# Log gates of a hybrid GLA/SSD layer: one fp32 array and fp32 masked sums in place of a high and a low part

## The chip, the core and the metric

The kernel runs on one core of a Trainium2 chip. The metric is the device time of one execution in microseconds; lower is better. Three timed runs of the kernel before gave 1431.48, 1432.50 and 1433.24 us, median 1432.5 us.

## What is computed

One layer of a diffusion backbone over 512 latent tokens and 256 context tokens, width 1024. A modulated RMS norm gives `h`; one input projection feeds a gated linear attention branch (GLA, 4 heads, two directions) and a state-space branch (SSD, 4 groups, two directions); both are projected back, gated, merged and added, and a SwiGLU FFN follows. The change concerns the log gates of GLA:

```
def log_gate(lr, up, bias):
    pre = (lr @ up + bias).astype(jnp.float32)
    return heads(jax.nn.log_sigmoid(pre) / GLA_TAU, GLA_DK)
# in the scan of a chunk:
b = jnp.cumsum(gi, axis=1)                  # running sum of the log gates
diff = b[:, :, None] - b[:, None, :]
decay = jnp.exp(jnp.where(mask, diff, -jnp.inf))
# the context's state, per head:
jnp.einsum('blhk,blhv->bhkv', k * jnp.exp(b[:, -1:] - b), v)
```

The sums over tokens (running sums within blocks of 128 tokens, and sums over what lies after or before a token) are matrix products with masks of zeros and ones.

## The kernel before

All matrices are cut into blocks of 512 KB that stream from DRAM on the queue of SyncE (`load_raw`, L173, three buffers `raw`). ScalarE rounds each to fp32r (`whi`, L188) and VectorE, or GpSimd in the SSD part, subtracts to get the rest (`wlo`, L189); there are two buffers of each. A projection is then three fp32r passes per product: high by high, high by low, low by high. The same three buffers `raw` also take blocks of the modulation weights (`raw_ada`), which GpSimd multiplies and adds up (L341 to L345).

The order of the instructions on each engine is made when the program is built: a list scheduler with a model of times places them, with priorities from the program order and from `tc.high_priority()`; each engine then executes its list in order and waits at semaphores. A tile of a pool with n buffers waits until the tile n before it of the same tag has been read.

The stretch in question follows the first projections. `MS` and `U` hold the low-rank gate input and its weights. For two directions `d` and six token tiles `i` (L466 to L480), TensorE makes `pre` (L469, PSUM bank of the kind `sm`, of which there are four), ScalarE takes Abs, Exp and Ln (L471 to L473), VectorE makes the log gate `ge` (`e` in the code, L474), rounds it to fp32r as `gh` (L477) and subtracts to get `gl` (L478). SyncE's queue writes both to a DRAM array `gdr` (L479, L480).

Then come the step sizes of SSD, "the dt stage" below: transposes `dtT` (L488) into two `sm` banks, `dt_v` (L489), a chain between VectorE and ScalarE through `dt_e`, `dt_u`, `dt_lu`, `dt_cr`, `dt` and `dt_ln` (L497 to L519), `nA` (L521), a load of ScalarE's tables for Tanh (L455), `dt_aH` and `dt_aL` (L527, L529), masked products `cum` and `suf` (L533), a copy `cum` (L541), `ebias` (L558), transposes and copies `cumT` (L562, L564). Beside it TensorE works on the projections: r of head 0 (`r_r`), then q and k of head 1 (`l_q`, and `l_k` with `c_k` for the context tokens).

`gla_chain(h)` (L582) handles one head. For each direction it loads the head's part of `gdr` on GpSimd's queue (L592, tiles `g` of the tags `cva` and `cvt`, two buffers each), makes running sums `gc` (four blocks), `kx` (384 columns) and `ky` (256 and 128 columns), each as one fp32r pass over the high part and one over the low part; all products with `early` have the line number L577. `gcum` and `kd` come from them. Level products `lv`, diagonal products `dg` and state products `S` are fp32 products already. In the program's text the projections of head h+1 stand behind the chain of head h; the scheduler interleaves them.

`ssd_chain(g)` (L784) follows the same pattern for four groups: `E` tiles are broadcast from DRAM on SyncE's queue (L829, tag `E4`, four buffers), added and merged on VectorE (L830, L832), and TensorE makes `st`, `y`, `yi` and the transposes `yT`, while the projections of the next group (`xs`, `z`) and the projection back (`pa`, `pb`) fill in.

Of the kernel before, what the change touches and what calls it, by code (L numbers as in the profile page):

```python
# [7 lines left out]
F32 = mybir.dt.float32  # L8
F32R = mybir.dt.float32r
I32 = mybir.dt.int32  # L10
U8 = mybir.dt.uint8
AF = mybir.ActivationFunctionType
ALU = mybir.AluOpType

P = 128
# [9 lines left out]
DK = 128  # L25
# [18 lines left out]
M_ID, M_LE, M_GE, M_GT, M_LT, M_ONE = range(6)  # L44
# [85 lines left out]
def hybrid_layer_kernel(ctx: ExitStack, tc: tile.TileContext, x, xc, wts, vec, rows, up, msk, lvl, out):  # L130
    nc = tc.nc
# [10 lines left out]
    dr = ctx.enter_context(tc.tile_pool(name="dr", bufs=1, space=DRAM))  # L142
# [4 lines left out]
    def sm_bank(name):  # L147
        return ps.tile([P, 512], F32, tag="sm", name=name)
# [4 lines left out]
    mkr = cst.tile([P, 5, P], F32R, name="mkr")  # L153
# [71 lines left out]
    with tc.tile_pool(name="st", bufs=1) as st:  # L225
# [77 lines left out]
        for i in range(6):  # L303
# [5 lines left out]
            for half in range(2):  # L309
                pt = sm_bank(f"xT_{i}_{half}")  # L310
# [9 lines left out]
    pj = mix.enter_context(tc.tile_pool(name="pj", bufs=2))  # L320
    ch = mix.enter_context(tc.tile_pool(name="ch", bufs=1))
# [27 lines left out]
    def proj_cols(key, with_ctx):  # L349
        if key[0] in ("q", "k") and key[1:2] != (0,):  # L350
            for _ in range(2):
                some_ada()
        if key[0] in ("ga", "gb"):
            some_ada()
        hi, lo = load_w(key)
        nm = "_".join(map(str, key))
        lat = mm_bank("l_" + nm)
        cx = mm_bank("c_" + nm) if with_ctx else None
        for k in range(KD):
            st, sp = k == 0, k == KD - 1  # L360
            nc.tensor.matmul(lat, hi[:, k, :], hH[:, k, 0:SEQ], start=st, stop=False)
            nc.tensor.matmul(lat, hi[:, k, :], hL[:, k, 0:SEQ], start=False, stop=False)
            if with_ctx:
                nc.tensor.matmul(cx[:, 0:CTX], hi[:, k, :], hH[:, k, SEQ:NT], start=st, stop=False)
                nc.tensor.matmul(cx[:, 0:CTX], hi[:, k, :], hL[:, k, SEQ:NT], start=False, stop=False)
            nc.tensor.matmul(lat, lo[:, k, :], hH[:, k, 0:SEQ], start=False, stop=sp)
            if with_ctx:
                nc.tensor.matmul(cx[:, 0:CTX], lo[:, k, :], hH[:, k, SEQ:NT], start=False, stop=sp)
        return lat, cx
# [91 lines left out]
        return gla_proj_vr(h, *gla_proj_qk(h))  # L461


    gdr = dr.tile([P, 2, 2, 6, 512], F32, name="gdr")

    for d in range(2):  # L466
        for i in range(6):
            pt = sm_bank(f"pre_{d}_{i}")
            nc.tensor.matmul(pt, MS[d][:, i * P:(i + 1) * P], U[:, d, :], start=True, stop=True)  # L469
            e = ch.tile([P, 512], F32, tag="s2", name=f"ge_{d}_{i}", bufs=7)  # L470
            nc.scalar.activation(e, pt, AF.Abs)  # L471
            nc.scalar.activation(e, e, AF.Exp, scale=-1.0)
            nc.scalar.activation(e, e, AF.Ln, bias=1.0)  # L473
            nc.vector.scalar_tensor_tensor(e, pt, 0.0, e, ALU.min, ALU.subtract)  # L474
            gh = ch.tile([P, 512], F32R, tag="z", name=f"gh_{d}_{i}", bufs=4)
            gl = ch.tile([P, 512], F32R, tag="E4", name=f"gl_{d}_{i}", bufs=4)
            nc.vector.tensor_copy(gh, e)  # L477
            nc.vector.tensor_tensor(gl, e, gh.bitcast(F32), ALU.subtract)  # L478
            nc.sync.dma_start(gdr[:, d, 0, i, :], gh.bitcast(F32))  # L479
            nc.sync.dma_start(gdr[:, d, 1, i, :], gl.bitcast(F32))  # L480


    dsh = [P, 6, 64]
# [1 line left out]
    for b, i0, n in ((0, 0, 4), (1, 4, 2)):  # L485
        pt = sm_bank(f"dtT_{b}")
# [6 lines left out]
    def dt_tile(name):  # L493
        return ch.tile(dsh, F32, tag="s2", name=name, bufs=7)

    e = dt_tile("dt_e")
# [63 lines left out]
    for d in range(2):  # L560
        pt = sm_bank(f"cumT_{d}")
# [6 lines left out]
    pr = gla_proj(0)  # L568


    class Early:


# [6 lines left out]
    early = Early()  # L580

    def gla_chain(h, qT, vt, kt, kT, rw, oH, oL):  # L582
        def s2(name, shape=(P, SEQ)):
            return ch.tile(list(shape), F32, tag="s2", name=f"{name}_{h}", bufs=7)

        cm, kd = [], []
        for d, mc, ms, n0, far, near in ((0, M_LE, M_GT, 0, 4, 5), (1, M_GE, M_LT, 1, 5, 4)):
            tag = ("cva", "cvt")[d]
            gp = []
            for p_ in range(2):  # L590
                gd = pj.tile([P, 6, DK], F32R, tag=tag, name=f"g_{h}_{d}_{p_}")
                nc.gpsimd.dma_start(gd, gdr[:, d, p_, :, h * DK:(h + 1) * DK])  # L592
                gp.append(gd)

            pt = sm_bank(f"gc_{h}_{d}")
            for n in range(NCH):
                for p_ in range(2):
                    early.matmul(pt[:, n * P:(n + 1) * P], gp[p_][:, n, :], mkr[:, mc - 1, :], start=(p_ == 0), stop=(p_ == 1))
            c_ = s2(f"gcum{d}")
            nc.scalar.activation(c_, pt, AF.Copy, scale=1.0 / TAU)  # L600
            cm.append(c_)

            px = sm_bank(f"kx_{h}_{d}")
            for p_ in range(2):
                early.matmul(px[:, 0:384], mkr[:, ms - 1, :], gp[p_][:, n0:n0 + 3, :], start=(p_ == 0), stop=(p_ == 1))
            py = sm_bank(f"ky_{h}_{d}")
            o0 = (far - 4) * P
            for p_ in range(2):
                early.matmul(py[:, 0:256], mkr[:, ms - 1, :], gp[p_][:, 4:6, :], start=(p_ == 0), stop=False)
            for p_ in range(2):  # L610
                early.matmul(py[:, o0:o0 + P], mkr[:, M_ONE - 1, :], gp[p_][:, near, :], start=False, stop=(p_ == 1))
            kk = pj.tile([P, 5, DK], F32, tag=tag, name=f"kd_{h}_{d}")
            nc.scalar.activation(kk[:, 0:3, :], px[:, 0:384].rearrange("p (i c) -> p i c", c=DK), AF.Exp, scale=1.0 / TAU)
            nc.scalar.activation(kk[:, 3:5, :], py[:, 0:256].rearrange("p (i c) -> p i c", c=DK), AF.Exp, scale=1.0 / TAU)
            nc.vector.tensor_tensor(kk[:, 0:3, :], kk[:, 0:3, :], kt[:, n0:n0 + 3, :], ALU.mult)
            nc.vector.tensor_tensor(kk[:, 3:5, :], kk[:, 3:5, :], kt[:, 4:6, :], ALU.mult)
            kd.append(kk)
# [12 lines left out]
        for d, order in ((0, (0, 1, 2, 3)), (1, (3, 2, 1, 0))):  # L630
            n0 = 0 if d == 0 else 1
            pt = sm_bank(f"S0_{h}_{d}")
# [3 lines left out]
            for a_, b_ in zip(order[:-1], order[1:]):  # L636
                pt = sm_bank(f"S_{h}_{d}_{b_}")
# [5 lines left out]
        pt = sm_bank(f"dg_{h}")  # L643
# [6 lines left out]
        for li, c in enumerate(LEVELS):  # L650
# [19 lines left out]
            pt = sm_bank(f"lv_{h}_{c}")  # L670
# [22 lines left out]
        for n in range(NCH):  # L693
# [4 lines left out]
            pt = pt2[:, (n % 2) * DV:(n % 2 + 1) * DV]  # L698
# [193 lines left out]

    oH0, oL0 = back_pair("oT_0")
    gla_chain(0, *pr, oH0, oL0)
    pr = gla_proj(1)
    gla_chain(1, *pr, oH0, oL0)
    pr = gla_proj(2)
    early_gate()
    proj_back(lambda c: ("pa", 0, c), oH0, oL0, acc_a, True)
    oH1, oL1 = back_pair("oT_1")  # L900
    gla_chain(2, *pr, oH1, oL1)
    pr = gla_proj(3)
    early_gate()
# [23 lines left out]
    for j in range(n_early[0], 8):  # L927
        ya = pj.tile([P, SEQ], F32, tag="cva", name=f"ya_{j}")
        nc.sync.dma_start(ya, ydr[:, j, :])
        lat, _ = proj_cols(("ga", j), False)  # L930
# [3 lines left out]
        lat, _ = proj_cols(("gb", j), False)  # L934
# [6 lines left out]
    pt = sm_bank("adaT")  # L941
# [72 lines left out]
    for i in range(4):  # L1014
# [14 lines left out]
        for half in range(2):  # L1029
# [3 lines left out]
            pt = sm_bank(f"hT_{i}_{half}")  # L1033
# [23 lines left out]
    for j0, nj in [(0, 2)] + [(j, 1) for j in range(2, NFF)]:  # L1057
# [12 lines left out]
        for j in js:  # L1070
            if nj == 2:
                f = sml.tile([P, SEQ], F32, tag="snw", name=f"f_{j}", bufs=1)
            else:
                f = fp.tile([P, SEQ], F32, tag="f32", name=f"f_{j}", bufs=2)
# [9 lines left out]
    pt = sm_bank("adaT2")  # L1084
# [130 lines left out]
```

## Time and profile before

| | value |
|---|---|
| median of three runs | 1432.5 us (1431.48 to 1433.24) |
| the profiled execution: its own time | 1428.55 us |
| its span, first to last instruction | 1426.7 us |
| TensorE busy | 1349.4 us (95%), 7462 products |
| VectorE busy | 881.1 us (62%) |
| ScalarE busy | 496.7 us (35%) |
| GpSimd busy | 476.1 us (33%) |
| mean granted TensorE clock | 0.986 of full speed |

The busy shares are means over stages that have different limits, so the rows are read by stretch: which engine is full there, and which wait of TensorE ends last. In a timeline row the numbers are start (us), length (us), engine, line, operation, and in brackets the idle time just before it on its engine with the instruction that ended it. Products are pipelined: the length of one holds its way through the array, so what a product costs TensorE is read from one start to the next, or from the length of a merged row (x8) against its count. An fp32 product appears as two records, an fp32r pass as one.

### The profile page before, as it was taken

How to read it: one execution, taken by the hardware profiler on the slowest of the kernel's cores; microseconds unless marked ns; L12 is line 12 of the kernel's file. 1: busy time of each engine (PE TensorE's matmuls, PEld its weight loads, DVE VectorE, ACT ScalarE, POOL GpSimd, SP SyncE). 2: the span in 40 equal slices, each digit the busy share in tenths (PEclk: the TensorE clock that was granted, in tenths of full speed). 3: DMA queues.
4: the chain of work that ended last, by engine and by line, in shares of the span. 5: the costliest groups of instructions: out<-in, count | busy, mean ns of one | idle time of the engine just before them, and what ended most of it. 6: DMA issues, size and time to landing. Idle time of an engine off the chain costs nothing.

```text
span 1426.7 us, 19130 instructions
## 1 busy us (share of the span) xinstructions
PE 1349.4 (95%) x7462; PEld 1146.0 (80%) x7462; DVE 881.1 (62%) x1317; ACT 496.7 (35%) x825; POOL 476.1 (33%) x341
## 2 busy tenths in 40 slices
PE   5888999999998999998999989999889999999997
PEld 3687999889888778876887787778678888888886
DVE  4599757583595588558857975767683343433235
ACT  6464343433434132532332342332333323232222
POOL 1346555245423533343353324114641122100001
PEclk9998999999999999999999999999999999999999
DMA  9375433423422423323322333457423343333331
GB/s 370 123 259 151 128 102 111 126 93 126 122 75 67 141 98 101 97 73 90 104 82 89 96 97 101 158 184 267 135 87 109 113 122 115 120 116 93 100 106 72
DMA packets 71386, 175.49 MB, mean 123 GB/s; under 512 B 6384, under 2 KB 22912, under 8 KB 71168
## 3 DMA queue, kind: packets, MB, share of 16 engines
q1 hardware_dynamic: 57056, 161.11, 34.6%
q0 software_dynamic: 13952, 12.79, 3.8%
q8 instruction: 59, 0.97, 0.3%
q10 hardware_dynamic: 288, 0.36, 0.1%
q14 instruction: 31, 0.25, 0.1%
HBM read 159.37 MB, written 14.87 MB: 122 GB/s over the span
## 4 chain that ended last, share of the span: by engine, by line
PE 66%; DVE 16%; DMA 9%; issue 5%; ACT 2%; POOL 1%; SPq 0%; POOLq 0%; DVEq 0%; ACTq 0%
DMA E<-cdr 6%; PE up L1069 3%; PE gate L1068 3%; PE gate L1069 3%; PE up L1068 3%; PE gate L1067 3%; PE up L1067 3%; DVE E L830 3%; PE db L204 3%; PE db L206 3%; PE db L205 3%; PE lv L577 2%; PE pb_pb L716 2%; PE pb_pb L715 2%; PE pb_pb L717 2%
## 5 line engine op out<-in xcount | busy, mean ns | idle before, releaser
L341 POOL TENSOR_TENSOR raw_ada<-raw_ada,cs 128x1024 f32<-128x1024 f32 x32 | 69.7, 2180 | 265.3 <-DMA raw_ada<-in_wts_dram 230.4
L830 DVE TENSOR_TENSOR E<-E,ebias 128x512 f32<-128x512 f32 x64 | 68.8, 1077 | 51.0 <-DMA E<-cdr 50.8
L343 POOL TENSOR_TENSOR raw_ada<-raw_ada 128x512 f32<-128x512 f32 x64 | 80.0, 1250 | 3.7
L386 PE MATMUL r_z<-whi_z,hH 128*128 128x256 f32 x256 | 74.6, 291 | 5.8 <-DVE z L781 3.0
L388 PE MATMUL r_z<-whi_z,hL 128*128 128x256 f32 x256 | 73.4, 287 | 0.0
L387 PE MATMUL r_z<-wlo_z,hH 128*128 128x256 f32 x256 | 73.0, 285 | 0.0
L1067 PE MATMUL gate<-h2H,whi_gate 128*128 128x512 f32 (+1 forms) x192 | 72.2, 376 | 0.0
L1068 PE MATMUL gate<-h2L,whi_gate 128*128 128x512 f32 (+1 forms) x192 | 72.1, 376 | 0.0
L1069 PE MATMUL gate<-h2H,wlo_gate 128*128 128x512 f32 (+1 forms) x192 | 71.9, 374 | 0.0
L189 POOL TENSOR_TENSOR wlo_xs<-raw_xs,whi_xs 128x1024 fp32r<-128x1024 f32 x16 | 40.6, 2536 | 75.3 <-ACT whi_xs L188 75.3
L1069 PE MATMUL up<-h2H,wlo_up 128*128 128x512 f32 x160 | 63.0, 394 | 0.0
L1068 PE MATMUL up<-h2L,whi_up 128*128 128x512 f32 x160 | 62.4, 390 | 0.0
L1067 PE MATMUL up<-h2H,whi_up 128*128 128x512 f32 x160 | 62.3, 389 | 0.0
L189 DVE TENSOR_TENSOR wlo_down<-raw_down,whi_down 128x1024 fp32r<-128x1024 f32 x18 | 22.1, 1225 | 62.4 <-ACT whi_down L188 62.3
L189 DVE TENSOR_TENSOR wlo_gate<-raw_gate,whi_gate 128x1024 fp32r<-128x1024 f32 x20 | 31.7, 1584 | 45.6 <-ACT whi_gate L188 45.6
L170 POOL TENSOR_TENSOR rr_f<-rv_f,negh 128x1 f32<-128x1 f32 x4 | 2.6, 662 | 168.5 <-DVE rv_f L168 168.5
L386 PE MATMUL r_v<-whi_v,hH 128*128 128x256 f32 x192 | 56.4, 294 | 0.0
L189 POOL TENSOR_TENSOR wlo_z<-raw_z,whi_z 128x1024 fp32r<-128x1024 f32 x16 | 39.6, 2475 | 49.2 <-ACT whi_z L188 36.6
L387 PE MATMUL r_v<-wlo_v,hH 128*128 128x256 f32 x192 | 55.5, 289 | 0.0
L715 PE MATMUL pb_pb<-yT,whi_pb 128*128 128x512 f32 x128 | 55.3, 434 | 0.0
L388 PE MATMUL r_v<-whi_v,hL 128*128 128x256 f32 x192 | 55.3, 288 | 0.0
L205 PE MATMUL db<-wlo_down,fH 128*128 128x512 f32 x142 | 55.3, 389 | 0.0
(479 smaller groups left out, 4446.7 us busy)
## 6 DMA issues: line engine op xcount, KB each, us to landing
raw_ada<-in_wts_dram SPq DMA_DIRECT2D x32, 512.0 KB, 4.0
E<-cdr SPq DMA_DIRECT2D x64, 256.0 KB, 3.5
raw_gate<-in_wts_dram SPq DMA_DIRECT2D x22, 512.0 KB, 3.7
raw_up<-in_wts_dram SPq DMA_DIRECT2D x22, 512.0 KB, 3.5
raw_down<-in_wts_dram SPq DMA_DIRECT2D x22, 512.0 KB, 3.5
aw<-in_wts_dram SPq DMA_DIRECT2D x8, 1024.0 KB, 15.5
raw_xs<-in_wts_dram SPq DMA_DIRECT2D x16, 512.0 KB, 3.5
raw_z<-in_wts_dram SPq DMA_DIRECT2D x16, 512.0 KB, 3.6
```

Source lines behind the costliest of these rows:

```text
L189: (nc.gpsimd if split_pool[0] else nc.vector).tensor_tensor(lo, raw, hi.bitcast(F32), ALU.subtract)
L205: nc.tensor.matmul(out_, aH, bL, start=False, stop=False)
L341: nc.gpsimd.tensor_tensor(raw, raw, cs[:, :, 0:1].to_broadcast([P, KD, P]), ALU.mult)
L343: nc.gpsimd.tensor_tensor(raw[:, 0:n, :], raw[:, 0:n, :], raw[:, n:2 * n, :], ALU.add)
L386: nc.tensor.matmul(o, hH[:, kk, tk], hi[:, k, :], start=st, stop=False, skip_group_check=True)
L387: nc.tensor.matmul(o, hH[:, kk, tk], lo[:, k, :], start=False, stop=False, skip_group_check=True)
L388: nc.tensor.matmul(o, hL[:, kk, tk], hi[:, k, :], start=False, stop=sp, skip_group_check=True)
L715: nc.tensor.matmul(pt, hi[:, k, cl], aH[:, k, :], start=(k == 0), stop=False)
L830: nc.vector.tensor_tensor(ed, ed, ebias[:, d, n, hh].unsqueeze(2).to_broadcast([P, EH, P]), ALU.add)
L1067: nc.tensor.matmul(pts[kj][:, tk], hi[:, k, :], h2H[:, k, tk], start=(k == 0), stop=False)
L1068: nc.tensor.matmul(pts[kj][:, tk], hi[:, k, :], h2L[:, k, tk], start=False, stop=False)
L1069: nc.tensor.matmul(pts[kj][:, tk], lo[:, k, :], h2H[:, k, tk], start=False, stop=(k == KD - 1))
```

## The change

The log gate is written once, as fp32, and read once. `gh`, `gl` and their tiles are gone; `gdr` has half the size; each masked sum is one fp32 product whose mask is the same array read as fp32. Nothing else is edited (`gates_end` is set and not used).

```
-    gdr = dr.tile([P, 2, 2, 6, 512], F32, name="gdr")
+    gdr = dr.tile([P, 2, 6, 512], F32, name="gdr")
...
-            nc.scalar.activation(e, e, AF.Ln, bias=1.0)
+            gates_end = nc.scalar.activation(e, e, AF.Ln, bias=1.0)
             nc.vector.scalar_tensor_tensor(e, pt, 0.0, e, ALU.min, ALU.subtract)
-            gh = ch.tile([P, 512], F32R, tag="z", name=f"gh_{d}_{i}", bufs=4)
-            gl = ch.tile([P, 512], F32R, tag="E4", name=f"gl_{d}_{i}", bufs=4)
-            nc.vector.tensor_copy(gh, e)
-            nc.vector.tensor_tensor(gl, e, gh.bitcast(F32), ALU.subtract)
-            nc.sync.dma_start(gdr[:, d, 0, i, :], gh.bitcast(F32))
-            nc.sync.dma_start(gdr[:, d, 1, i, :], gl.bitcast(F32))
+            nc.sync.dma_start(gdr[:, d, i, :], e)
...
+    def mkf(m):
+        return mkr[:, m - 1, :].bitcast(F32)
...
-            gp = []
-            for p_ in range(2):
-                gd = pj.tile([P, 6, DK], F32R, tag=tag, name=f"g_{h}_{d}_{p_}")
-                nc.gpsimd.dma_start(gd, gdr[:, d, p_, :, h * DK:(h + 1) * DK])
-                gp.append(gd)
+            gd = pj.tile([P, 6, DK], F32, tag=tag, name=f"g_{h}_{d}")
+            nc.gpsimd.dma_start(gd, gdr[:, d, :, h * DK:(h + 1) * DK])
...
-                for p_ in range(2):
-                    early.matmul(pt[:, n * P:(n + 1) * P], gp[p_][:, n, :], mkr[:, mc - 1, :], start=(p_ == 0), stop=(p_ == 1))
+                early.matmul(pt[:, n * P:(n + 1) * P], gd[:, n, :], mkf(mc), start=True, stop=True)
...
-            for p_ in range(2):
-                early.matmul(px[:, 0:384], mkr[:, ms - 1, :], gp[p_][:, n0:n0 + 3, :], start=(p_ == 0), stop=(p_ == 1))
+            early.matmul(px[:, 0:384], mkf(ms), gd[:, n0:n0 + 3, :], start=True, stop=True)
...
-            for p_ in range(2):
-                early.matmul(py[:, 0:256], mkr[:, ms - 1, :], gp[p_][:, 4:6, :], start=(p_ == 0), stop=False)
-            for p_ in range(2):
-                early.matmul(py[:, o0:o0 + P], mkr[:, M_ONE - 1, :], gp[p_][:, near, :], start=False, stop=(p_ == 1))
+            early.matmul(py[:, 0:256], mkf(ms), gd[:, 4:6, :], start=True, stop=False)
+            early.matmul(py[:, o0:o0 + P], mkf(M_ONE), gd[:, near, :], start=False, stop=True)
```

The scheduler makes a new order from it. Three places of it matter below. The first is the end of the gates and the start of the dt stage. On VectorE there stand before (the number behind a name is a serial number; line numbers behind L480 are lower in the changed kernel):

```order
L474 SCALAR_TENSOR_TENSOR ge_4_608<-pre_4_606,ge_4_608 128x512
L474 SCALAR_TENSOR_TENSOR ge_5_621<-pre_5_619,ge_5_621 128x512
L477 CAST gh_4_613<-ge_4_608 128x512
L215 TENSOR_TENSOR ada<-ada_1060,vecs 128x1
L489 TENSOR_TENSOR dt_v<-dtT_639,early_in 128x128
L477 CAST gh_5_626<-ge_5_621 128x512
L478 TENSOR_TENSOR gl_4_614<-ge_4_608,gh_4_613 128x512
L478 TENSOR_TENSOR gl_5_627<-ge_5_621,gh_5_626 128x512
L500 TENSOR_SCALAR dt_u<-dt_e 128x384
L505 SCALAR_TENSOR_TENSOR dt_cr<-dt_u,dt_e 128x384
L189 TENSOR_TENSOR wlo_q_1397<-raw_q_1398,whi_q_1396 128x1024
```

and in the changed kernel, on the same engine at the same place:

```order
L474 SCALAR_TENSOR_TENSOR ge_4_558<-pre_4_556,ge_4_558 128x512
L474 SCALAR_TENSOR_TENSOR ge_5_566<-pre_5_564,ge_5_566 128x512
L484 TENSOR_TENSOR dt_v<-dtT_579,early_in 128x128
L215 TENSOR_TENSOR ada<-ada_1000,vecs 128x1
L189 TENSOR_TENSOR wlo_q_1319<-raw_q_1320,whi_q_1318 128x1024
L495 TENSOR_SCALAR dt_u<-dt_e 128x384
L500 SCALAR_TENSOR_TENSOR dt_cr<-dt_u,dt_e 128x384
L501 TENSOR_SCALAR dt_e<-dt_e 128x384
```

The roundings and subtractions are gone, and `wlo_q` now stands ahead of `dt_u`. On ScalarE at this place, before:

```order
L497 ACTIVATE dt_e<-dt_v 128x384
L498 ACTIVATE dt_e<-dt_e 128x384
L188 ACTIVATE whi_q_1396<-raw_q_1398 128x1024
L502 ACTIVATE dt_lu<-dt_u 128x384
L516 ACTIVATE dt_ln<-dt_u 128x384
L521 ACTIVATE nA<-early_in 128x64
L455 ACT_TABLE_LOAD
```

and in the changed kernel:

```order
L188 ACTIVATE whi_q_1318<-raw_q_1320 128x1024
L492 ACTIVATE dt_e<-dt_v 128x384
L493 ACTIVATE dt_e<-dt_e 128x384
L497 ACTIVATE dt_lu<-dt_u 128x384
L188 ACTIVATE whi_k_1362<-raw_k_1364 128x1024
L511 ACTIVATE dt_ln<-dt_u 128x384
L516 ACTIVATE nA<-early_in 128x64
L455 ACT_TABLE_LOAD
```

`whi_q` moved ahead of the dt stage, and `whi_k` of head 1, which stood behind it, now stands inside it, ahead of `dt_ln`. The second place is TensorE around the transposes `cumT`, which end the dt stage, before:

```order
L533 MATMUL suf<-dt_aH,mkr 128x32
L533 MATMUL suf<-dt_aL,mkr 128x32
L562 MATMUL cumT_701<-idt,cum 128x128
L562 MATMUL cumT_706<-idt,cum 128x128
L441 MATMUL kt_0_799<-idt,kv_740 128x128 x4
L361 MATMUL l_k_1446<-hH,whi_k_1440 128x512
L362 MATMUL l_k_1446<-hL,whi_k_1440 128x512
L364 MATMUL c_k_1447<-hH,whi_k_1440 128x256
```

and in the changed kernel:

```order
L361 MATMUL l_k_1368<-hH,whi_k_1362 128x512
L362 MATMUL l_k_1368<-hL,whi_k_1362 128x512
L364 MATMUL c_k_1369<-hH,whi_k_1362 128x256
L365 MATMUL c_k_1369<-hL,whi_k_1362 128x256
L557 MATMUL cumT_641<-idt,cum 128x128
L557 MATMUL cumT_646<-idt,cum 128x128
L366 MATMUL l_k_1368<-hH,wlo_k_1363 128x512
L368 MATMUL c_k_1369<-hH,wlo_k_1363 128x256
L441 MATMUL kt_0_739<-idt,kv_680 128x128 x4
```

Passes of the k projection of head 1 moved ahead of `cumT`: 34 of its 48 stand between the first `cum` product and `cumT`, where before there was none. The third place is SyncE's queue where the SSD part begins, before:

```order
L176 DMA raw_z_0_0_4214<-in_wts_dram 128x1024
L176 DMA raw_z_0_1_4268<-in_wts_dram 128x1024
L176 DMA raw_z_1_0_4332<-in_wts_dram 128x1024
L829 DMA E_0_0_0_4626<-cdr 128x512
L829 DMA E_0_0_1_4629<-cdr 128x512
L176 DMA raw_z_1_1_4386<-in_wts_dram 128x1024
L829 DMA E_0_1_0_4634<-cdr 128x512
```

and in the changed kernel:

```order
L176 DMA raw_z_0_0_4082<-in_wts_dram 128x1024
L176 DMA raw_z_0_1_4136<-in_wts_dram 128x1024
L820 DMA E_0_0_0_4494<-cdr 128x512
L820 DMA E_0_0_1_4497<-cdr 128x512
L176 DMA raw_z_1_0_4200<-in_wts_dram 128x1024
L820 DMA E_0_1_0_4502<-cdr 128x512
L820 DMA E_0_1_1_4505<-cdr 128x512
L820 DMA E_1_0_0_4564<-cdr 128x512
L820 DMA E_1_0_1_4567<-cdr 128x512
L176 DMA raw_z_1_1_4254<-in_wts_dram 128x1024
```

The loads of `E` stand one or two weight blocks earlier; the same holds in the other three groups, and the chain's products on TensorE moved with them.

## Rows read from the trace of the kernel before

**Rows 1.** Busy time by stretch: us, engines' busy us, PEclk, DMA share, GB/s.

```profile
72.00:125.00 53.00, 44.70 (x304) 41.46 (x304) 50.71 (x70) 29.60 (x53) 27.18 (x24) 0.90 0.78 240
123.00:400.00 277.00, 274.49 (x1812) 252.71 (x1812) 179.41 (x313) 105.46 (x196) 134.25 (x101) 1.00 0.39 113
...
107.40:114.30 6.90, 5.09 (x12) 4.08 (x13) 6.37 (x13) 2.95 (x5) 2.79 (x2) 0.51 1.11 307
121.10:124.50 3.40, 3.40 (x15) 3.21 (x16) 3.40 (x5) 0.98 (x2) 1.88 (x3) 0.50 0.57 161
```

**Rows 2.** Timeline of TensorE, 95 to 121 us: its three waits.

```profile
95.48 0.66 PE L488 MATMUL dtT<-idt,M 128*128 128x128 f32 x4 [2.69 <-DVE ge L474]
...
109.21 0.80 PE L366 MATMUL l_q<-hH,wlo_q 128*128 128x512 f32 x1 [3.33 <-DVE wlo_q L189]
...
120.98 1.05 PE L441 MATMUL kt<-idt,kv 128*128 128x128 f32 x4 [2.01 <-DVE cumT L564]
```

**Rows 3.** VectorE by line, 60 to 125 us: count, busy us, mean ns, idle before.

```profile
L478 DVE TENSOR_TENSOR gl<-ge,gh 128x512 fp32r<-128x512 f32 x12 | 15.8, 1328 | 0.1
L477 DVE CAST gh<-ge 128x512 fp32r<-128x512 f32 x12 | 8.5, 713 | 0.1
L474 DVE SCALAR_TENSOR_TENSOR ge<-pre,ge 128x512 f32<-128x512 f32 x12 | 7.9, 682 | 0.0
```

**Rows 4.** Timeline of VectorE, 76 to 116 us: the gates' end and the dt stage.

```profile
76.68 0.69 DVE L478 TENSOR_TENSOR gl<-ge,gh 128x512 fp32r<-128x512 f32 x1
...
100.73 2.03 DVE L477 CAST gh<-ge 128x512 fp32r<-128x512 f32 x1
...
102.75 0.28 DVE L489 TENSOR_TENSOR dt_v<-dtT,early_in 128x128 f32<-128x128 f32 x1
...
103.28 3.62 DVE L478 TENSOR_TENSOR gl<-ge,gh 128x512 fp32r<-128x512 f32 x2
...
107.94 1.22 DVE L189 TENSOR_TENSOR wlo_q<-raw_q,whi_q 128x1024 fp32r<-128x1024 f32 x1
...
115.84 1.26 DVE L529 TENSOR_TENSOR dt_aL<-dt_a,dt_aH 128x384 fp32r<-128x384 f32 x1
```

**Rows 5.** TensorE by line and shape, whole span: the masked sums of the gates.

```profile
L577 PE MATMUL gc<-mkr,g 128*128 128x128 f32 x64 | 10.6, 277 | 0.0
...
L577 PE MATMUL kx<-g,mkr 128*128 128x384 f32 x16 | 5.5, 376 | 0.0
...
L577 PE MATMUL ky<-g,mkr 128*128 128x256 f32 x16 | 3.5, 283 | 0.0
L577 PE MATMUL ky<-g,mkr 128*128 128x128 f32 x16 | 3.5, 272 | 0.0
```

**Rows 6.** Timeline of TensorE: merged runs of fp32r passes and of fp32 products.

```profile
144.06 1.05 PE L577 MATMUL dg<-qT,kv 128*128 128x128 f32 x8
...
270.01 1.06 PE L577 MATMUL gc<-mkr,g 128*128 128x128 f32 x8
...
275.44 1.46 PE L577 MATMUL S<-kv,kd 128*128 128x256 f32 x6
278.58 1.02 PE L577 MATMUL S<-kv,kd 128*128 128x256 f32 x4
...
374.25 0.22 PE L577 MATMUL gc<-mkr,g 128*128 128x128 f32 x1
374.31 0.65 PE L577 MATMUL S<-kv,kd 128*128 128x256 f32 x2
```

**Rows 7.** The chain that ended last, at 1380 us: six passes of 512 columns.

```profile
1380.89 1.36 PE db L204 x6
```

**Rows 8.** Waits of TensorE, whole span: total us, times, longest.

```profile
PE yT L577 <- DVE y L866: 9.8, 6, 1.9
```

**Rows 9.** Waits of SyncE's queue, 400 to 920 us: total us, times, longest.

```profile
SPq L829 <- DVE E L832: 128.7, 24, 9.4
```

**Rows 10.** DMA issues of the page: count, KB each, us to landing.

```profile
raw_xs<-in_wts_dram SPq DMA_DIRECT2D x16, 512.0 KB, 3.5
```

## The prediction

> **What bounds the kernel now.** I read the busy time by stretch first, since the whole-span shares hide where an engine is full [rows 1]. From 123 to 400 us, where all four GLA chains run, TensorE is busy 274.5 of 277.0 us: work that lands on it there lengthens the span, and work taken from another engine there brings nothing. From 72 to 125 us it is the other way round: VectorE is busy 50.7 of 53.0 us and TensorE only 44.7. TensorE's timeline then says what it waits for [rows 2]: 2.69 us for `ge`, 3.33 us for `wlo_q`, 2.01 us for `cumT`, 8.0 us together, each time ended by VectorE. Behind the second and the third wait the granted clock is at half, 1.2 in place of 2.4 GHz: 0.51 from 107.4 to 114.3 us and 0.50 from 121.1 to 124.5 [rows 1]. TensorE is busy 5.09 and 3.40 us there, and at full clock the same work takes half of that, so the low clock costs 2.5 + 1.7 = 4.2 us. The front thus holds 8.0 + 4.2 = 12.2 us that a freer VectorE could give back at most.
>
> **The roundings and subtractions that go.** `gl` takes 15.8 us and `gh` 8.5 us of VectorE between 60 and 125 us [rows 3], together 24.3 of the 50.7 us, in the stretch where it is full. Without them it would be busy some 26 of 53 us, and TensorE's own 44.7 us, less the 4.2 us of low clock, become the larger.
>
> Part of the 24.3 us is not work. One `gl` takes 0.69 us at 76.68 us [rows 4] and 1.33 us on average, while `ge`, which reads one operand from PSUM, always takes about its 0.68 us [rows 3]. The Trainium skill (SBUF — State Buffer, "Who interferes with whom") says that a VectorE instruction with two SBUF inputs and a GpSimd instruction that reads SBUF lock each other out. By that rule some of the waiting only moves to the next two-input instruction, and VectorE saves as little as 24 x 0.69 = 16.6 us, an estimate with that length for `gl` and `gh` alike; even so it would be busy 34 of 53 us, below TensorE, and the sum would be the same.
>
> How much of the 12.2 us comes back is decided by what is late next, the dt stage. Before, the second `dt_v` starts at 102.75 us and `dt_aL` ends at 115.84 + 1.26 = 117.1 us, 14.35 us later [rows 4]. Two `gl` (3.62 us) inside go; one weight split of the size of `wlo_q` (1.22 us) comes in, because `wlo_k` now stands there: about 12.0 us. `dt_v` itself stood 7.3 us behind the start of `dtT` (95.48 us), of which the `gh` of 2.03 us goes [rows 2, 4]: 5.3 us. So `dt_aL` ends some 17.3 us after `dtT`. TensorE, without waits, needs from `dtT` to the end of q: 109.21 - 3.33 - 95.48 = 10.4 us up to where it waited, and then the 22 of q's 24 passes that were left, at 1.36 / 6 = 0.227 us each [rows 2, 7], 5.0 us: 15.4 us. It arrives about 1.9 us early. Part of that is filled, since only the first two masked products are ahead of the k projection now and they need `dt_aH` alone. I leave 2.2 us of the 12.2 in place, the gap with a little low clock, and take **10.0 us** as the gain of the front. The wait for `ge` goes because `dtT` needs a PSUM bank that `ge` frees, and `ge` no longer queues behind `gh` and `gl`; the wait for `wlo_q` goes because nothing but `dt_v` stands ahead of it; the wait for `cumT` goes because 34 passes of k now cover it. Bounds: 12.2 us if nothing is left, 2.7 us if only the wait for `ge` goes.
>
> **The products that change form.** Per head and direction there are four `gc`, one `kx` and two `ky`, 56 products in all, and 112 passes before [rows 5]; an fp32 product is two records, so 112 remain. At 128 columns nothing changes: eight passes of `gc` take 1.06 us, and eight records of `dg`, four fp32 products of the same shape, 1.05 us [rows 6]. Above that the columns count. An fp32r pass costs 0.227 us at 512 columns, 0.44 ns a column [rows 7]; an fp32 record costs (1.46 - 1.02) / 2 = 0.22 us at 256, 0.86 ns a column [rows 6]. A product of n columns so goes from 0.89 n to 1.72 n ns: 0.32 us more for `kx`, 0.21 us for the wide `ky`. Eight times 0.53 is **4.3 us more on TensorE**, inside the stretch where it is full, so on the path. Bounds: between other work one pass of `gc` takes only 374.31 - 374.25 = 0.06 us [rows 6], and if all 40 products of 128 columns went from twice that to 0.22 us, 4.0 us more, 8.3 us; if the 2.5 us that TensorE idles from 123 to 400 us [rows 1] hid their part, 1.8 us. A gain is excluded, since no product has fewer columns or records.
>
> **What moves aside.** Twelve writes and eight reads of gates go; no wait of TensorE that I found was ended by them. SyncE's queue gains most: the loads of `raw_q` and `raw_k` no longer queue behind writes that wait for `gl`. GpSimd issues eight loads fewer and `g` needs one buffer in place of two; nothing on the path waits there, so nothing is counted. In the SSD part the same instructions run in another order; I take 0 us with 6 us to either side, and treat both signs below.
>
> **The sum.** -10.0 + 4.3 = -5.7 us. The profiled execution took 1428.55 us and would take 1422.9; it lies 3.95 us under the median of the runs, 1432.5, so the runs should show **1426.8 us**.
>
> **The rivals.** Differences under 0.2%, 2.9 us, count as no change; that is about what a measurement here can tell.
>
> *A, the forecast*, chance 0.50: front 7 to 12, products 1.8 to 8.3, mostly 1424 to 1430 us.
>
> *B, the gain of the front is covered*, 0.22: `whi_k` now stands inside the dt stage on ScalarE, ahead of `dt_ln`, `nA` and the table load. If `raw_k` lands late, ScalarE waits, all of these queue behind it, and TensorE waits at `cum` for `dt_aH`. The waits for `wlo_q` and `cumT` with the first low clock, 3.33 + 2.01 + 2.5 = 7.8 us, then come back under another name; 12.2 - 7.8 = 4.4 us remain and the products eat 4.3: 1432.4 us. For it: the three `raw` buffers are shared with GpSimd's slow `raw_ada` blocks. Against it: `raw_k` takes the buffer of `raw_q`, which `wlo_q` frees early now.
>
> *C, slower through the new order in SSD*, 0.12: loads of `E` stand ahead of one or two weight blocks on SyncE's queue, and they wait for their buffer: 128.7 us in 24 waits, up to 9.4 us [rows 9]. A weight block behind such a wait starts late. If once in each of the four groups TensorE runs out of weights for the 3.5 us that a block needs to land [rows 10], that is 14 us: 1432.5 - 5.7 + 14 = 1440.8 us. It decides once an `E` wait is longer than what the two split blocks in hand last. Against it: before, no wait of TensorE in SSD was for weights.
>
> *D, the new order helps*, 0.12: more projection passes now stand inside each SSD chain, where TensorE waited 9.8 us for `y` ahead of `yT` alone [rows 8]; with 6 us of such waits filled, 1420.8 us.
>
> *E, fp32 costs twice an fp32r pair throughout*, 0.04: then all 112 passes' time doubles, 80 x 0.11 + 16 x 0.17 + 16 x 0.114 = 13.3 us, and the sum is +3.3: 1435.8 us. The equal times of `gc` and `dg` speak against it [rows 6]. The Trainium skill (FP8 and Floating Point Precision, "TensorE Precision Notes") gives true fp32 four passes through the array, which against two would be this case; the trace agrees with it only above 128 columns.
>
> **How the numbers follow.** Faster: nearly all of A and D, 0.60. Same: B and the rest of A, 0.24. Slower: C and E, 0.16. The likeliest case gives 1426.8 us. The range for 8 in 10 reaches from a little below D, 1419.5, past B to E, 1436; it leaves out C and the tail beyond D.
>
> **What would show it.** In the changed kernel's page, VectorE should be about 24 us less busy, from 72 to 125 us well under 40. The three waits of rows 2 should be gone or small, and the clock full from 105 to 125 us. `kx` should take 0.6 to 0.7 us for two records, `gc` unchanged. B shows as a wait of ScalarE's `whi_k` for its load and a wait of TensorE's `cum`; C as waits of TensorE for `whi` or `wlo` of `xs`, `z` or `pb`; D as fewer waits of `yT`. The prediction is wrong if the front's waits only change their name, or if SSD's waits move by more than 6 us.

## The result, and the profile after

The changed kernel takes 1442.8 us (median of four runs, 1440.4 to 1444.7), the kernel before, run beside it, 1432.0 us: a ratio of 1.0073, with a 95% interval of 1.0046 to 1.0100. By the ratio that is 10.5 us slower (10.8 by the medians), where 5.7 us faster was forecast; 1442.8 lies 6.8 us above the upper end of the range, 1436. The profiled execution took 1441.4 us, with a mean granted clock of 0.979 in place of 0.986.

Busy time by stretch of the changed kernel, with the columns of [rows 1]:

```profile
72.00:125.00 53.00, 47.84 (x331) 44.42 (x330) 32.59 (x46) 28.63 (x52) 32.57 (x26) 0.94 0.55 184
123.00:400.00 277.00, 268.11 (x1733) 244.28 (x1732) 171.90 (x306) 103.94 (x193) 119.66 (x91) 0.98 0.30 97
109.70:116.50 6.80, 4.24 (x11) 3.47 (x12) 6.55 (x7) 3.05 (x6) 5.63 (x5) 0.50 0.35 133
195.00:201.80 6.80, 4.20 (x20) 4.21 (x21) 3.85 (x9) 1.64 (x4) 2.37 (x4) 0.50 0.32 97
```

The front did much of what was forecast: VectorE's 50.7 us from 72 to 125 us have become 32.6 [rows 1]. The loss stands in the second row. In the stretch where TensorE had been busy all but 2.5 of 277 us, it now idles 8.9 us, and its clock is 0.98 in place of 1.00. (The stretches are cut by time, so they do not hold exactly the same work in both kernels.) One wait is new there and comes three times, as TensorE's waits from 120 to 300 us show (total us, times, longest):

```profile
PE oT L575 <- DVE on L686: 6.8, 3, 4.7
```

The timelines of TensorE, VectorE and GpSimd give the chain behind the long one (start, length, engine, line, operation, idle before and what ended it). TensorE, with two rows from the front:

```profile
112.26 0.48 PE L528 MATMUL cum<-dt_aH,mkr 128*128 128x128 f32 x1 [3.82 <-ACT dt_aH L522]
...
122.40 0.60 PE L441 MATMUL kt<-idt,kv 128*128 128x128 f32 x4
...
197.60 0.69 PE L575 MATMUL oT<-idt,on 128*128 128x128 f32 x2 [4.70 <-DVE on L686]
```

VectorE:

```profile
188.61 0.17 DVE L168 TENSOR_SCALAR rv_o<-oss 128x4 f32<-128x4 f32 x1 [5.08 <-ACT on L682]
197.06 1.66 DVE L686 SCALAR_TENSOR_TENSOR on<-o,rr_o,rw 128x256 f32<-128x256 f32 x4 [8.28 <-POOL rr_o L170]
```

GpSimd:

```profile
187.01 0.73 POOL L343 TENSOR_TENSOR raw_ada<-raw_ada 128x256 f32<-128x256 f32 x1
191.98 1.90 POOL L341 TENSOR_TENSOR raw_ada<-raw_ada,cs 128x1024 f32<-128x1024 f32 x1 [4.25 <-DMA raw_ada<-in_wts_dram]
193.96 2.06 POOL L343 TENSOR_TENSOR raw_ada<-raw_ada 128x512 f32<-128x512 f32 x2
195.98 1.04 POOL L170 TENSOR_TENSOR rr_o<-rv_o,negh 128x4 f32<-128x4 f32 x1
```

`rr_o`, the inverse root of the norm of head 0's output, is 128x4 and takes 1.04 us on GpSimd. Its input `rv_o` is there at 188.8 us. But on GpSimd's queue a block of modulation weights stands ahead of it, and that block's load lands only at 192. So `rr_o` starts at 196 us; `on` waits for it, `oT` for `on`, and the clock is at half from 195.0 to 201.8 us. On a smaller scale the same happens to head 1: `rv_o` is there at 264.9 us, an instruction of 1.90 us on modulation weights runs ahead of `rr_o`, `oT` waits 1.63 and 0.43 us at 267 to 269 us, and the clock is at half from 270.1 to 273.5. Before, `rr_o` of head 0 stood ahead of that block, whose load landed just as late. GpSimd's timeline of before:

```profile
187.88 1.04 POOL L170 TENSOR_TENSOR rr_o<-rv_o,negh 128x4 f32<-128x4 f32 x1
191.67 2.71 POOL L341 TENSOR_TENSOR raw_ada<-raw_ada,cs 128x1024 f32<-128x1024 f32 x1 [2.75 <-DMA raw_ada<-in_wts_dram]
```

This place is not among the three shown in the section on the change.

### The profile page after: what moved, and what is told of

The parts are those of the page before. It is cut to its first block, busy times and chain, and to the rows that moved or that the text cites. A ratio compares the mean times of both kernels' runs of the same rounds, so it can differ in the third digit from the quotient of the medians.

```text
span 1439.6 us, 19045 instructions
## 1 busy us (share of the span) xinstructions
PE 1358.3 (94%) x7462; PEld 1154.0 (80%) x7462; DVE 873.3 (61%) x1293; ACT 498.7 (35%) x825; POOL 470.1 (33%) x333
## 4 chain that ended last, share of the span: by engine, by line
PE 63%; DVE 15%; DMA 9%; issue 6%; POOL 4%; ACT 2%; SPq 1%; POOLq 0%; DVEq 0%; ACTq 0%
DMA E<-cdr 4%; PE up L1060 3%; PE gate L1059 3%; PE gate L1060 3%; PE gate L1058 3%; PE up L1059 3%; PE up L1058 3%; PE db L204 3%; PE db L206 3%; PE db L205 3%; DVE E L821 2%; PE lv L575 2%; PE pb_pb L706 1%; PE pb_pb L708 1%; PE pb_pb L707 1%
## 5 line engine op out<-in xcount | busy, mean ns | idle before, releaser
L821 DVE TENSOR_TENSOR E<-E,ebias 128x512 f32<-128x512 f32 x64 | 51.8, 815 | 44.0 <-DMA E<-cdr 43.8
L343 POOL TENSOR_TENSOR raw_ada<-raw_ada 128x512 f32<-128x512 f32 x64 | 76.7, 1198 | 3.9
L386 PEld LDWEIGHTS r_z<-whi_z,hH 128*128 128x128 f32 x256 | 49.9, 196 | 8.5 <-DVE z L772 5.5
```

The costliest lines, as they stand in the source:

```text
L343: nc.gpsimd.tensor_tensor(raw[:, 0:n, :], raw[:, 0:n, :], raw[:, n:2 * n, :], ALU.add)
L386: nc.tensor.matmul(o, hH[:, kk, tk], hi[:, k, :], start=st, stop=False, skip_group_check=True)
L821: nc.vector.tensor_tensor(ed, ed, ebias[:, d, n, hh].unsqueeze(2).to_broadcast([P, EH, P]), ALU.add)
```

## The experiments

The theories: (1) the loss comes from the new order that the scheduler made, above all from `rr_o`; (2) the fp32 products cost far more than their rows say; (3) TensorE, early after the shorter front, meets a limit in any order. To hold the order fixed or to move single instructions, the kernels carry a table with the order of every engine, and each instruction is tied behind the one ahead of it; the work is not touched:

```
+    text = {i.name: i for i in nc.cur_bb.bb.instructions}
...
+        for p_, q_ in zip(row, row[1:]):
+            tc.add_manual_dep(q_, p_.name, no_sync, reason="order")
```

Times are given as ratios to the kernel before, run beside each. Ratios of different rounds are compared by their difference, times 1432 us, and their intervals are added in squares.

**e9, the control.** The changed kernel with its own order in the table.

> The changed kernel with its own order written out, nothing else: what e1 differs from by two places on GpSimd. If writing out the order costs nothing, it gives the changed kernel's ratio to the kernel before, 1.007 (1.0046 to 1.010 when it was first timed), and lies some 12 us above e1.

Measured 1.0074 (1.0052 to 1.0096), and `oT` waits 4.68 us again. The table costs nothing that can be seen.

**e1.** One place on GpSimd for head 0, one for head 1:

```
-L341 raw_ada, L343, L343, L170 rr_o
+L170 rr_o, L341 raw_ada, L343, L343
```

> The changed kernel with the order of every engine written out as it is, except on GpSimd: rr_o of heads 0 and 1 stands ahead of the nearest block of modulation weights (raw_ada) in place of behind it. Theory 1 (the loss comes from the new order: rr_o, a 128x4 instruction, is queued on GpSimd behind a block whose load lands late, VectorE's on waits for it, TensorE's oT for on): the waits of oT at 193 and 267 us, 4.70 + 1.63 us, go, and with them the low clock behind them (195.0 to 201.8 and 270.1 to 273.5 us, 10.2 us at half, 5.1 us of work lost): about 10 us less, 1433. Theory 2 (the fp32 products cost far more than their rows say): no change, 1442.8. Theory 3 (TensorE arrives early after the shorter front and meets a limit whatever the order): the wait takes another name in the same stretch, 1440 or more.

Measured 0.9986 (0.9967 to 1.0005): 12.6 +- 4 us less than e9. GpSimd's timeline in e1:

```profile
189.99 1.04 POOL L170 TENSOR_TENSOR rr_o<-rv_o,negh 128x4 f32<-128x4 f32 x1 [1.29 <-DVE rv_o L168]
193.03 2.99 POOL L341 TENSOR_TENSOR raw_ada<-raw_ada,cs 128x1024 f32<-128x1024 f32 x1 [1.99 <-DMA raw_ada<-in_wts_dram]
```

TensorE's waits in e1 from 120 to 300 us:

```profile
PE lv L575 <- DVE ek L658: 1.2, 1, 1.2
PE oT L575 <- DVE on L686: 0.3, 1, 0.3
```

The block still waits for its load, but nothing waits for the block. Theory 1 holds for the GLA stage, and 3 falls there.

**e5, the reverse.** The kernel before, with `rr_o` of head 0 behind the next block.

> The kernel before, every engine in its own order, but on GpSimd rr_o of head 0 stands behind the next block of modulation weights in place of ahead of it: it would end some 9 us later, at 198 in place of 188.9 us. Theory 1 (a late rr_o holds on, on holds oT, TensorE stands still and its clock falls): oT, which stood 1 us behind on, waits about 8 us, with up to 3.4 us for the low clock behind it: 8 to 11 us more than the kernel before, a ratio of 1.0055 to 1.008. Theory 3 (an early TensorE meets a limit in any order; one late step is absorbed): within 0.2% of the kernel before.

Measured 1.0046 (1.0022 to 1.0070), 6.6 us more: less than the 8 to 11 us expected, though the interval, 3.2 to 10.0 us, reaches into them. GpSimd's timeline in e5:

```profile
195.62 1.04 POOL L170 TENSOR_TENSOR rr_o<-rv_o,negh 128x4 f32<-128x4 f32 x1
```

TensorE's in e5:

```profile
197.24 0.69 PE L577 MATMUL oT<-idt,on 128*128 128x128 f32 x2 [6.56 <-DVE on L695]
```

and e5's busy time in the stretch behind, with the columns of [rows 1]:

```profile
193.80:200.60 6.80, 3.36 (x14) 3.26 (x15) 3.52 (x8) 1.48 (x4) 2.87 (x4) 0.50 0.27 79
```

A wait of 6.56 us in place of the 8 I expected, and the low clock. One instruction's place in a queue is enough for the wait.

**e2.** The changed kernel's work, all of it in the order of before.

> The changed kernel's instructions in the order of the kernel before on every engine, from first to last; a product of the gates stands where its first pass stood. Theory 1 (the new order loses): the waits for ge and wlo_q with one low clock go, 2.7 + 3.3 + 2.5 = 8.5 us at most, the wait for cumT stays since k does not cover it, the products add 4.3, nothing is lost from 150 us on: 1428 to 1432. Theory 2 (the products cost far more): 1440 or more. Theory 3 (an early TensorE waits in any order): the front's gain is lost in the GLA chains, 1436.

Measured 0.9947 (0.9926 to 0.9969): 7.6 us faster than before, which is 1424.4 us by the ratio and better than the 1428 to 1432 expected. Theory 2 falls: with the same products the change is a gain.

**e3 and e4.** Own order to 131 us, then the old one; e4 besides with two fp32r passes:

```
+            gp = [gd.bitcast(F32R)] * 2
```

> The changed kernel's instructions in its own order up to 131 us on every engine, and behind that in the order of the kernel before. Theory 1 (the new order loses): the front's 8.6 us stay, the products add 4.1 to 4.3, nothing else: 1432.0 - 8.6 + 4.2 = 1427.6. Theory 2 (the products cost far more): 1440. Theory 3 (an early TensorE meets a limit in any order): 8.6 us come back as waits before 400 us, 1436.

> As the kernel before this one in order (own order to 131 us, then the old one), but each product of the gates is again two fp32r passes, both over the one array (the low part is left out and the high part counted twice, so that its sums are another value). Against that kernel it isolates the price of the products. Theory 1: 4.1 to 4.3 us less, 1423.4. Theory 2 (the products cost far more): 10 us less or more. If the 128-column products cost the same in both forms, only kx (0.32) and the wide ky (0.21) differ, eight times each.

Measured 0.9991 (0.9979 to 1.0003) and 0.9956 (0.9942 to 0.9971). Their difference, 5.0 +- 2.7 us, is the products' price in this order, and e4 says what the front brings in its own order, the join of the two orders included: 6.3 us (4.2 to 8.3). e3 misses its 1427.6 by some 3 us: where the two orders join, the state products `S` wait 1.65 us at 135 us, with 3.4 us at half clock behind. It tells less than e2 for that.

**e12 and e13.** Each part alone, in exactly the old order.

> The products alone, with every engine in exactly the order of the kernel before: roundings, subtractions, writes and loads stay, and each product of the gates is one fp32 product over the high part (the low part is loaded and not used). No order changes, so the difference is the price of the products alone: 8 x (0.32 + 0.21) = 4.3 us by the rows (1.8 to 8.3), 5.0 us by e3 against e4: a ratio to the kernel before of 1.003 to 1.0035. If their price is what made e7 lose, 1.009.

> The front alone, with every engine in the order of the kernel before: the gates are written and read once, without roundings and subtractions; each product is two fp32r passes over the one array (the low part left out, the high part counted twice). The wait for ge and that for wlo_q should go, the wait for cumT stay in part: 7 to 8 us by the traces of e1 to e3, and by e2 (0.9947) with the products' 4.3 to 5 us taken off, 12 us: a ratio of 0.991 to 0.995.

Measured 1.0019 (0.9997 to 1.0040), 2.7 us more, and 0.9958 (0.9939 to 0.9976), 6.0 us less. The front brings less than the 7 to 12 us that I expected from e1 to e3. Together the two give -3.3 us, e2 gave -7.6; the intervals meet, and the forecast -5.7 lies between. Read as a difference, e2 less e13, the products would cost -1.6 +- 4.1 us.

**e6 and e7.** Each part alone, in the order that the scheduler makes for it. e6 is e13's kernel without its table, e7 is e12's.

> One part of the change alone: the gates written and read once, without roundings and subtractions, but the products still two fp32r passes each, both over the one array (the low part left out, the high part counted twice). The scheduler makes its own order; it again puts rr_o of head 0 behind a block of modulation weights on GpSimd. Theory 1 (order): it keeps the loss, and lies below the changed kernel only by the price of the products, 4 to 5 us: a ratio to the kernel before of 1.003 to 1.005. Theory 2 (the fp32 products make the loss): the front's gain alone, ratio 0.994.

> The other part alone: roundings, subtractions, writes and loads as in the kernel before, but each product one fp32 product over the high part (the low part is loaded and not used). The scheduler makes its own order; rr_o of heads 0 and 1 does not stand behind a waiting block in it. By their price the products add 4 to 5 us, a ratio of 1.003; the new order of SSD adds or takes what it did there between the changed kernel and e1, 1 to 5 us: 1.003 to 1.007 in all. Theory 2 (the products make the whole loss): 1.009 or more, with the front's gain missing.

Measured 1.0111 (1.0086 to 1.0135) and 1.0090 (1.0066 to 1.0115). Both are worse than I expected, by 9 us (e6) and 3 us (e7) beyond the upper end. Against e13 and e12, which differ from them in order alone, the order costs 21.9 and 10.2 us. e7 has no wait of `oT` for `rr_o` in GLA, so there is a second loss. The next two look for it in the SSD part.

**e10 and e11.** e10 is e1 to 440 us, then the old order; e11 is the kernel before to 440 us, then the new order.

> As e1 up to 440 us on every engine (own order, rr_o of heads 0 and 1 ahead), and behind that, through the SSD part to the end, the order of the kernel before. Theory 1a (rr_o explains GLA, and the new order of SSD loses besides): 2 to 8 us less than e1, a ratio to the kernel before of 0.993 to 0.997. Theory 1b (rr_o is all of it, the order of SSD does not matter): as e1, 0.9986, within 0.2%.

> The kernel before, with its own order up to 440 us and behind that, through the SSD part to the end, the order of the changed kernel; the work is that of the kernel before. Theory 1a (the new order of SSD loses): 2 to 10 us more than the kernel before, a ratio of 1.0015 to 1.007. Theory 1b: 1.000, within 0.2%.

Measured 0.9944 (0.9923 to 0.9965), 6.0 +- 4 us less than e1, and 1.0060 (1.0039 to 1.0082), 8.6 us more than before. Theory 1a holds. e10 beats both kernels, as e2 does.

One thing that the SSD order does is seen on VectorE. Its row for `y` by line, from 460 to 860 us (count, busy us, mean ns, idle before), in the kernel before:

```profile
L866 DVE SCALAR_TENSOR_TENSOR y<-y,rr_y,snw 128x512 f32<-128x512 f32 x12 | 8.9, 743 | 1.0 <-POOL rr_y L170 1.0
```

in the changed kernel:

```profile
L857 DVE SCALAR_TENSOR_TENSOR y<-y,rr_y,snw 128x512 f32<-128x512 f32 x12 | 20.6, 1714 | 3.6 <-POOL rr_y L170 3.6
```

in e10, old order:

```profile
L857 DVE SCALAR_TENSOR_TENSOR y<-y,rr_y,snw 128x512 f32<-128x512 f32 x12 | 11.1, 924 | 1.5 <-POOL rr_y L170 1.5
```

and in e11, new order:

```profile
L866 DVE SCALAR_TENSOR_TENSOR y<-y,rr_y,snw 128x512 f32<-128x512 f32 x12 | 17.0, 1416 | 3.6 <-POOL rr_y L170 3.6
```

One of these in the changed kernel's timeline, on VectorE:

```profile
688.01 2.82 DVE L857 SCALAR_TENSOR_TENSOR y<-y,rr_y,snw 128x512 f32<-128x512 f32 x1 [0.39 <-POOL rr_y L170]
```

on GpSimd:

```profile
687.94 2.33 POOL L189 TENSOR_TENSOR wlo_z<-raw_z,whi_z 128x1024 fp32r<-128x1024 f32 x1
```

and on TensorE:

```profile
690.97 0.41 PE L575 MATMUL yT<-idt,y 128*128 128x128 f32 x2 [2.90 <-DVE y L857]
```

And one in the timeline of before, on VectorE:

```profile
575.39 0.75 DVE L866 SCALAR_TENSOR_TENSOR y<-y,rr_y,snw 128x512 f32<-128x512 f32 x1 [0.33 <-POOL rr_y L170]
```

and on GpSimd:

```profile
576.72 2.39 POOL L189 TENSOR_TENSOR wlo_z<-raw_z,whi_z 128x1024 fp32r<-128x1024 f32 x1 [1.36 <-issue]
```

In the new order GpSimd begins `wlo_z` 0.07 us ahead of `y`, and `y` takes 2.82 us in place of 0.75; before, `wlo_z` began after `y` had ended. Of the twelve, six take 2.1 to 2.9 us in the changed kernel, each beside a weight subtraction of GpSimd that began between 1.0 us ahead of it and 0.03 us behind; the other six take 0.74 to 0.76 us, as all twelve did before. `y` is what the transposes `yT` wait for. This was read in the traces and not tried by moving that one `wlo_z`. The Trainium skill (SBUF — State Buffer, "Who interferes with whom") says that only a port pair that VectorE and GpSimd share causes contention, as an exclusive lock; these rows fit it.

The waits of TensorE through SSD in sum are hardly more in the new order. I added up its idle times over 0.15 us from 460 to 860 us, and the spells at half clock that begin there:

```
order of SSD   kernel          waits us  longest us  half clock us
old            before            23.2      1.89          3.4
old            e2                23.5      1.89          3.4
old            e10               21.6      1.88          6.8
old            e12               23.4      1.89          3.4
new            changed           22.5      2.90         13.7
new            e1                23.1      3.02          6.8
new            e9                23.1      2.82         17.1
new            e11               23.8      2.74         13.7
own            e6                29.1      3.21         20.5
own            e7                25.3      2.99         17.1
```

(e3, e4, e5 and e13, in the old order too, lie at 21.2 to 23.2 us of waits and 3.4 us at half clock, e8, in the new one, at 24.0 and 13.7.) In the old order no wait is over 1.9 us. The new one holds about as much waiting, but with single waits of 2.7 to 3.0 us, and the clock is at half for longer; e1's trace is the exception, with 6.8 us as in e10. 10.3 us more at half clock, as between before and e11, cost some 5 us of work.

Not all of these low clocks hang on `y`. In e11 the longest wait of `yT`, 2.74 us at 691.6 us, has none behind it. The longest spell there, from 850.7 us, comes with a wait of `r_z` for `z`, and `z` stands on VectorE behind an `E` that waits for its load, as `rr_o` stood behind `raw_ada`. VectorE in e11:

```profile
850.25 0.69 DVE L830 TENSOR_TENSOR E<-E,ebias 128x512 f32<-128x512 f32 x1 [2.45 <-DMA E<-cdr]
851.46 0.41 DVE L781 SCALAR_TENSOR_TENSOR z<-z,r_z 128x256 f32<-128x256 f32 x1
```

TensorE in e11, and the busy time of the stretch, with the columns of [rows 1]:

```profile
851.93 0.58 PE L386 MATMUL r_z<-whi_z,hH 128*128 128x256 f32 x1 [2.73 <-DVE z L781]
850.70:857.50 6.80, 5.57 (x26) 5.57 (x27) 5.96 (x12) 4.72 (x10) 2.37 (x1) 0.50 0.01 3
```

ScalarE had the input of this `z` ready at 848.5 us. Before, `r_z` waits 1.57 us at this place, and no low clock follows. Moving this `z` was not tried either. So that the order of SSD loses is shown, but how the loss divides between `y`, `z` and other waits is not.

The times of the runs point to the clock as well. A run's time multiplied by its mean granted clock is about what it would take at full clock (an estimate). On average e1's twelve runs took 1432.2 us at 0.9818, which gives 1406.1, and e10's six 1424.0 us at 0.9875, which gives 1406.2: as far as these averages tell, what e10 gains on e1 is all in the clock. For e11 and the kernel before beside it the products are 1410.9 and 1408.5 us: 2.4 of the 8.3 us between their means are outside the clock.

**e8.** e1, with the first `cum` and `suf` product behind 16 passes of k, and `wlo_k` earlier, to fill the 4.47 us that TensorE waits there in e1 for `dt_aH`.

> As e1 (own order, rr_o of heads 0 and 1 ahead), and at the end of the front two moves more: the first cum and the first suf product stand behind the 16 k passes that followed them, and wlo_k of head 1 ahead of dtb on VectorE. In e1 TensorE waits 4.47 us there for dt_aH and runs 6.8 us at half clock behind it. If the k passes cover that wait, it and 3.4 us of low clock go: about 7 us less than e1, a ratio to the kernel before of 0.994. If wlo_k then comes late in place of dt_aH, no more than 2 us are won.

Measured 1.0033 (1.0013 to 1.0054), 6.7 +- 4 us worse than e1, where 7 us better was expected. TensorE's timeline in e8:

```profile
115.16 0.80 PE L361 MATMUL l_k<-hH,whi_k 128*128 128x512 f32 x1 [6.18 <-DVE rw L456]
```

It was neither of the two waits that I named: `whi_k` was ready at 109.0 us, but `l_k` waits for `rw`. `rw` reads the results of r of head 0; I take it that `l_k` needs the PSUM bank these hold. On ScalarE `rw` stands behind `dt_ln` and the load of the tables. So in this order q and k cannot cover the dt stage to its end.

## Why the prediction was wrong

- **What bounds the kernel: right**, and it names the price of the miss. From 123 to 400 us TensorE was full, so each wait put there counts in whole.
- **The roundings and subtractions: right in kind.** VectorE is 18.1 us less busy from 72 to 125 us, not 24. The low estimate by the Trainium skill (SBUF — State Buffer, "Who interferes with whom"), 16.6 us, is the nearer one there: part of the waiting moved, as that rule has it. The two `wlo_r` from 60 to 135 us, with two SBUF inputs each, rose from 1214 to 1941 ns on average. Over the whole span VectorE saves 20.1 us in the old order (881.1 us before, 861.0 in e2) but only 7.8 in the changed kernel (873.3), since the new order of SSD makes its instructions longer by 8.6 us (289.3 to 297.9 us from 460 to 860 us, 444 each).
- **The front: right in sign, 4 us too large.** 10.0 us were forecast; e13 measured 6.0 (3.4 to 8.7) in the old order and e4 6.3 (4.2 to 8.3) in the new one. The waits for `ge`, `wlo_q` and `cumT` are gone: the changed kernel's timeline shows none ahead of `dtT`, q or `kt`. But I left 2.2 us for what comes next, and it was 3.82 us at `cum` for `dt_aH`, with the clock at 0.50 from 109.7 to 116.5 us. That the clock would be full from 105 to 125 us was wrong; it was 0.83. In e13's old order `cum` waits 2.2 and 1.1 us there and, behind the front, `S` 3.7 us for `kd`. What holds `dt_aH` in the new order is what rival B named. In the changed kernel's chain that ended last, the load of `raw_k`:

```profile
102.00 4.72 DMA raw_k<-in_wts_dram
```

  and in ScalarE's timeline:

```profile
106.80 1.06 ACT L188 ACTIVATE whi_k<-raw_k 128x1024 fp32r<-128x1024 f32 x1 [4.49 <-DMA raw_k<-in_wts_dram]
```

  In that chain GpSimd's work on `raw_ada` ends at 101.54 us, only then SyncE's queue goes on to `raw_k`, and `whi_k`, `dt_ln`, `dt_a`, `dt_aH` and `cum` follow one another.
- **The products: right within their bounds.** 4.3 us were forecast; e12 measured 2.7 (-0.4 to 5.7), e3 against e4 5.0 (2.3 to 7.7), e2 against e13 -1.6 (-5.7 to 2.5). The changed kernel's groups by shape:

```profile
L575 PE MATMUL gc<-mkr,g 128*128 128x128 f32 x64 | 10.6, 296 | 0.5 <-DMA g<-gdr 0.5
L575 PE MATMUL kx<-g,mkr 128*128 128x384 f32 x16 | 6.6, 495 | 0.0
L575 PE MATMUL ky<-g,mkr 128*128 128x256 f32 x16 | 4.8, 379 | 0.0
L575 PE MATMUL ky<-g,mkr 128*128 128x128 f32 x16 | 3.1, 274 | 0.0
```

  `gc` is unchanged [rows 5]. From one start to the next two records of `kx` take 0.65 us:

```profile
370.61 0.81 PE L575 MATMUL kx<-g,mkr 128*128 128x384 f32 x2
371.26 0.39 PE L575 MATMUL gc<-mkr,g 128*128 128x128 f32 x2
```

  as forecast. An old pass of `kx` between other work took 0.23 us, not the 0.17 of its columns, as TensorE's timeline of before shows:

```profile
368.70 0.39 PE L577 MATMUL kx<-g,mkr 128*128 128x384 f32 x1
368.93 0.56 PE L577 MATMUL gc<-mkr,g 128*128 128x128 f32 x4
```

  The rival that fp32 costs twice a pair throughout (13.3 us, and more with the 0.13 us of [rows 6] in place of the 0.11 that it takes for a pass of 128 columns) is excluded by e12. The Trainium skill (FP8 and Floating Point Precision, "TensorE Precision Notes") gives true fp32 four passes; at 128 columns no run here shows more than the time of two.
- **The sum: its number holds in the old order.** -5.7 was forecast, e2 measured -7.6 (-10.6 to -4.4). That is in part luck: the sum counts on passes of k that cover `cumT`, which stand there only in the new order, and alone both parts came out smaller, 6.0 and 2.7 us.
- **What moves aside: the step that failed.** It said of GpSimd that nothing on the path waits there, and of SSD "I take 0 us with 6 us to either side". GpSimd carries `rr_o`, on which `oT` hangs, and the new order put it behind a block whose load was still under way: 12.6 us by e9 against e1. VectorE's waits for `rr_o` were in the trace of before (9.7 us in four), but there TensorE had other work. I looked at the order at three places, none of them on GpSimd's queue, and not at all at GLA behind the front. The order of SSD costs 6.0 (e10) to 8.6 us (e11), at or above the end of my 6. In sum: 8.0 us gained (e10), 6.0 and 12.6 lost, 10.6 us slower; these three lead from the kernel before by e10 and e1 to e9, so that they add up is no check. The sign that I gave for an error in SSD, waits that move by more than 6 us, would not have shown it: their sum went from 23.2 to 22.5 us, while the time at half clock went from 3.4 to 13.7.
- **The rivals.** C had the sign and the place in SSD, but not the cause: TensorE waits for weights 1 us there (`l_xs` for `whi_z`), not 14. B came true in its place and by its mechanism, `whi_k` waiting for `raw_k` and `cum` for `dt_aH`; the front lost about half of what B gave for it, 4 of 7.8 us. D's waits of `yT` fell a little, from 9.8 to 8.4 us, but SSD as a whole went the other way.

## What to carry to other kernels

Where a scheduler sets the order, an edit's own price can be smaller than that of the order it brings about: here 3 to 8 us gained and 19 us lost. Before trusting a sum made with the old order, follow each small instruction on a full engine's chain, here `rr_o`, through every queue that it stands in, and ask what is ahead of it and whether that waits for a load. The traces here show the pattern three times: `dt_ln` behind `whi_k`, `rr_o` behind `raw_ada`, `z` behind `E`. Only `rr_o` was moved to prove it (e1, e5). To judge an edit, time it in the old order as well; if the edit is good and the order is not, keep the edit and pin the few instructions that matter (e1, e10).

## What was not expected of the hardware

- Equal sums of waiting cost unequal time: in the table of SSD, e6 and e7 left aside, the waits lie between 21.2 and 24.0 us and the time at half clock between 3.4 and 17.1.
- The same program scatters with its clock: in e1 the four runs at a mean clock of 0.984 or 0.985 took 1427.6 to 1431.4 us, the eight at 0.980 to 0.982 took 1428.8 to 1438.0. One trace alone does not settle a difference of 5 us.
- A VectorE instruction of 0.75 us took 2.82 us beside a GpSimd instruction of 2.33 us. Which of the two begins first is a matter of the order, and the two-input instructions that are hit change with it: from 460 to 860 us `E` with `ebias` fell from 1124 to 826 ns on average, while `y` rose from 743 to 1714.
